# Hybrid decoder block on one core: high-part products first at the head of both networks, squares added in pairs

## The chip, the cores and the metric

The kernel runs on one core of a Trainium2 chip. The metric is the device time of one execution in microseconds (us); the time before is the median of three runs. The engines are TensorE (PE in the rows; its weight loads PEld), VectorE (DVE), ScalarE (ACT), GpSimd (POOL) and SyncE (SP), which issues most DMAs.

## What is computed

A decoder block on 1040 tokens (16 meta tokens and 1024 inputs) of width 1024: a gated network, a middle part, a second gated network, and a last normalization.

```python
def _rmsnorm(x, gain):
    xf = x.astype(jnp.float32)
    y = xf * lax.rsqrt(jnp.mean(xf * xf, axis=-1, keepdims=True) + EPS)
    return (y * gain.astype(jnp.float32)).astype(x.dtype)
def _swiglu(x, w_gu, w_down):
    gate, up = jnp.split(x @ w_gu, 2, axis=-1)
    return (jax.nn.silu(gate) * up) @ w_down
...
h = h + 0.5 * _swiglu(_rmsnorm(h, ffn1_norm[l]), ffn1_w_gu[l], ffn1_w_down[l])
...
h = h + merged @ w_out[l]
h = h + 0.5 * _swiglu(_rmsnorm(h, ffn2_norm[l]), ffn2_w_gu[l], ffn2_w_down[l])
return _rmsnorm(h, final_norm)[:, N_META:]
```

The middle part (a chunked delta-rule branch and an RWKV-7 branch, merged) is not touched. `w_gu` has 2 x 2816 columns, so each network has 22 blocks of 128 gate columns and 22 of up columns, over a contraction of 8 tiles of 128.

## The kernel before

**Products.** A float32 product is made as three products of rounded parts: `split` (L159, L160) makes a high copy on ScalarE and the low rest, source minus high, on VectorE, and TensorE sums high by high, high by low and low by high in PSUM. Weights go through `split` too (`w<-wraw`, `w<-wrx`).

**The networks.** Activations lie with the 1024 features on partitions (8 tiles, `KD`; `HK` = 4 is half of them) and the tokens along the free axis, in two halves of n tokens: n is 520 in the first network (as 256 and 264 columns, `halves`) and 512 in the second. A tile of the first half is called `h` (first network) or `hh` (second); its split form is `b` (`11` and `21`: tiles 0 to 3 and 4 to 7), that of the second half is `12` and `22`, `bt` and `b` in the rows. `gate_up` (L474 and on) does the first pair of units with `plain`: for each half h of the tokens four products (gate of unit 0, gate of unit 1, up of both), each 24 matmuls for every stretch of columns, in an order of all three parts of a tile, tile by tile. Each product has its own PSUM tile (`pg`). From the second pair on `product` (L450) does fewer products by combining halves; its first matmuls are the end of the head.

**The norm.** `rstd` squares a tile on ScalarE (L318), sums over the partitions by a matmul with ones (L320; float32, two records a matmul in the trace, PSUM tile `nps`), over all eight tiles, and makes 1/sqrt by Ln and Exp (L323, L324) into `nrs`. `first_half` multiplies each tile by gain and `nrs` on VectorE (L336) and splits it; `second_half` does the same for the other half (L354). In the second network the statistics of the first half come from elsewhere (L293).

**The order.** `start` interleaves the generators: weights, second half's norm, products. A scheduler places instructions on the engines from that order and from when their inputs should be ready, so parts of the norm lie among products of `plain`. In the second network the products of the attention output (`pwo`, L262) lie on TensorE just ahead; their weights are split by the same two engines, and VectorE adds them up at L898. The tiles of squares, `nrs` and the gates share a pool of six (`ga`). The first loads of `h` go alternately over ScalarE's and SyncE's queues (L648).

Of the kernel before, what the change touches and what calls it, by code (L numbers as in the profile page):

```python
# [300 lines left out]
    return g.ga.tile([P, n], F32, name=name, tag="ga", bufs=6)  # L301


def rstd(g, src, n, on_pe):

    nc = g.nc
    new = lambda: ga_tile(g, n, "nsq")
    if not on_pe:
        r = Rms(g, new, n)
        for k in range(KD):  # L310
            r.add(src(k))
        rs = g.ga.tile([P, n], F32, name="nrs", tag="nrs")
        r.finish(rs)
        return rs
    ps = [g.mx.tile([P, 512], F32, name="nps", tag="mx")[:, :cn] for _, cn in halves(n)]
    for k in range(KD):
        t = new()
        nc.scalar.activation(t, src(k), AF.Square)  # L318
        for p, (c0, cn) in zip(ps, halves(n)):
            nc.tensor.matmul(p, lhsT=g.C("ones"), rhs=t[:, c0 : c0 + cn], start=k == 0, stop=k == KD - 1)  # L320
    rs = ga_tile(g, n, "nrs")
    for p, (c0, cn) in zip(ps, halves(n)):
        nc.scalar.activation(rs[:, c0 : c0 + cn], p, AF.Ln, bias=g.V("eps"), scale=1.0 / D)  # L323
    nc.scalar.activation(rs, rs, AF.Exp, scale=-0.5)  # L324
    return rs
# [4 lines left out]
def first_half(g, hs, gname, n, b, on_pe):  # L330

    src = lambda k: hs[k][:, :n]
    rs = rstd(g, src, n, on_pe)
    yield
    for k in range(KD):
        g.nc.vector.scalar_tensor_tensor(src(k), src(k), g.V(gname, k), rs, op0=ALU.mult, op1=ALU.mult)  # L336
        bk = b["21" if k >= HK else "11"][:, k % HK]
        split(g, src(k), bk[:, 0, :], bk[:, 1, :])
    yield


# [95 lines left out]
def gate_up(g, which, n, w, b):  # L437
# [26 lines left out]
        add(c11, c12, p2)  # L464
        return w, c12, c11

    def plain(l1, r1, l2, r2):
        ps = mm_tile(g, "pg", n)
        for c0, cn in halves(n):
            i = 0  # L470
            for l, r in ((l1, r1), (l2, r2)):
                for k in range(HK):
                    for x, y in ((0, 0), (0, 1), (1, 0)):
                        nc.tensor.matmul(ps[:, c0 : c0 + cn], lhsT=l[:, x, k, :], rhs=r[:, k, y, c0 : c0 + cn],  # L474
                                         start=i == 0, stop=i == 6 * HK - 1)
                        i += 1
        return ps

    def store(x, p, h):
        nc.sync.dma_start(g.hid[p + HF * (h // 2)][:, h % 2 * n : (h % 2 + 1) * n], x)  # L480

    for h in range(2):
        gate = []
        for u in w:
            for m in range(2):
                ps = plain(u[f"{m + 1}1"], b[f"1{h + 1}"], u[f"{m + 1}2"], b[f"2{h + 1}"])
                if len(gate) < 2:
                    x = ga_tile(g, n, "c")
                    nc.scalar.activation(x, ps, AF.Silu)
                    gate.append(x)  # L490
                else:
                    x = gate[m]
                    nc.vector.tensor_tensor(x, ps, x, op=ALU.mult)
                    store(x, 0, 2 * m + h)
        yield
# [116 lines left out]
        f0 += G  # L612


def start(g, which, hs, gname, n, b, w, q):

    more = second_half(g, hs, gname, n, b)
    gu = g.gate_up = gate_up(g, which, n, w, b)
    next(q)
    next(more)  # L620
    next(q)
    next(gu)
    next(more)
# [8 lines left out]
def ffn1(g):  # L632
    tc, nc = g.tc, g.nc
    n = T // 2
    with ExitStack() as ctx:
# [7 lines left out]
        with tc.tile_pool(name="f1n", bufs=1, reuse_waits="tile") as sp:  # L643
            hs = [sp.tile([P, T], F32, name=f"h{k}") for k in range(KD)]
            for s in range(2):
                for k in range(KD):
                    sl = slice(s * n, (s + 1) * n)
                    (nc.sync if s or k % 2 else nc.scalar).dma_start(hs[k][:, sl], g.a["hT"][k][:, sl])  # L648
                if not s:
                    weight_tiles(g)  # L650
                    q0 = whole(g, 1, 0, 0, g.wq[0], g.wq[1])
                    w0 = next(q0)
# [4 lines left out]
            next(q0)  # L657
            next(first)
            next(q0)
            start(g, 1, hs, "g1", n, b, (w0, w1), q1)  # L660
            gu = g.gate_up
        hidden = Hidden(g, ctx.enter_context(tc.tile_pool(name="f1d", bufs=1, reuse_waits="tile")), T)
        with tc.tile_pool(name="gs", bufs=1, reuse_waits="tile") as sp:
# [1032 lines left out]
```

## Time and profile before

| | |
|---|---|
| median of three runs | 3088.84 us (3085.60 to 3089.95) |
| the profiled execution | 3085.29 us, span 3083.5 us, mean granted clock 0.989 |
| TensorE busy | 2959.3 us, 96% of the span |
| VectorE busy | 1976.2 us, 64% |
| ScalarE busy | 1376.7 us, 45% |
| first matmul of a product, first network | 20.30 us |
| first matmul of the second pair of units, first network | 71.90 us |
| first matmul of the first pair, second network | 2394.80 us |
| first matmul of the second pair, second network | 2438.77 us |

All times count from the start of the profiled execution's span. A row of a timeline is a run of instructions of the same kind on one engine: start, length, engine, line, operation, output and input, how many, and in brackets how long the engine stood idle ahead of it and who ended that. The granted clock is given as a share of full speed.

### The profile page before, as it was taken

The page shows a single profiled execution, that of the slowest core. Times are in us where ns is not written, and L with a number is a line of the kernel's source. Part 1 is how long each engine was busy: PE and PEld are TensorE (multiplying, and loading weights), DVE is VectorE, ACT ScalarE, POOL GpSimd, SP SyncE. Part 2 cuts the span into 40 slices and gives each one's busy share as a digit, 9 for nine tenths or more (in the row PEclk, how much of TensorE's full clock was granted, in tenths as well). Part 3 has the DMA queues.
Part 4 walks back from the last instruction along what each step waited for, and adds up shares of the span by engine and source line. Part 5 has one row for each costly group of instructions (what it writes and reads, how often), then busy time and mean ns, then how long its engine had stood idle before and what let it go on. Part 6 is the DMA issues. An engine that isn't in the chain of part 4 may idle for free.

```text
span 3083.5 us, 61656 instructions
## 1 busy us (share of the span) xinstructions
PE 2959.3 (96%) x25498; PEld 2539.0 (82%) x25498; DVE 1976.2 (64%) x3840; ACT 1376.7 (45%) x2404; POOL 354.9 (12%) x519
## 2 busy tenths in 40 slices
PE   8999999999899999999999999999999999999998
PEld 8999998998778888788777777777777888887886
DVE  6455454346677777787867877777866655555335
ACT  5322222126555656566566655665644432222114
POOL 0222220000001000001001000010100022222000
PEclk9999999999899999999999999999999999999999
DMA  3232224234222322333332332223354232224223
GB/s 125 82 97 83 83 86 158 79 101 140 62 74 73 79 70 59 85 79 75 97 89 73 84 81 75 75 75 84 109 148 165 68 104 94 83 83 170 86 78 114
DMA packets 257593, 287.19 MB, mean 93 GB/s; under 512 B 169296, under 2 KB 175440, under 8 KB 257312
## 3 DMA queue, kind: packets, MB, share of 16 engines
q1 hardware_dynamic: 253072, 271.43, 29.4%
q0 software_dynamic: 2512, 8.65, 0.7%
q8 instruction: 201, 3.29, 0.4%
q10 hardware_dynamic: 1728, 3.16, 0.3%
q14 instruction: 80, 0.66, 0.1%
HBM read 232.70 MB, written 50.47 MB: 92 GB/s over the span
## 4 chain that ended last, share of the span: by engine, by line
PE 54%; DVE 11%; ACT 7%; issue 2%; DMA 2%; SPq 0%; DVEq 0%; POOL 0%; ACTq 0%
PE pp L262 18%; PE pg L450 12%; PE pd L262 7%; PE pwo L262 3%; DVE w L160 1%; PE pg L474 1%; PE b L1542 1%; PE cs L1003 1%; PE gra L1252 1%; DMA ugr<-in_upg 1%; PE bkt L1281 1%; DVE tb L1364 1%; DVE mt L1472 1%; DVE Xb L1366 1%; PE vp L1056 1%
## 5 line engine op out<-in xcount | busy, mean ns | idle before, releaser
L262 PE MATMUL pp<-uk,w 128*128 128x512 f32 (+2 forms) x4824 | 975.1, 347 | 15.8 <-DVE w L160 9.3
L262 PEld LDWEIGHTS pp<-uk,w 128*128 128x128 f32 x4824 | 744.7, 191 | 109.1 <-DVE w L160 13.0
L159 ACT ACTIVATE w<-wraw 128x1024 fp32r<-128x1024 f32 (+2 forms) x330 | 326.3, 989 | 712.6 <-PE pd L262 287.6
L262 PE MATMUL pd<-hd,w 128*128 128x512 f32 (+2 forms) x2640 | 495.6, 349 | 11.3 <-DVE w L160 6.7
L262 PEld LDWEIGHTS pd<-hd,w 128*128 128x128 f32 x2640 | 427.5, 189 | 78.2 <-DVE w L160 8.6
L160 DVE TENSOR_TENSOR w<-wraw,w 128x1024 fp32r<-128x1024 f32 (+2 forms) x330 | 376.1, 1140 | 90.9 <-ACT w L159 85.7
L456 DVE TENSOR_TENSOR c<-c,pg 128x520 f32<-128x520 f32 (+1 forms) x280 | 189.2, 689 | 337.3 <-PE pg L450 278.3
L450 PE MATMUL pg<-bt,w 128*128 128x256 f32 (+2 forms) x2520 | 403.9, 317 | 0.0
L450 PEld LDWEIGHTS pg<-bt,w 128*128 128x128 f32 x2520 | 361.0, 188 | 32.9 <-DVE w L160 0.2
L450 PE MATMUL pg<-b,w 128*128 128x256 f32 (+2 forms) x2160 | 348.1, 317 | 0.2 <-DVE c L456 0.2
L450 PEld LDWEIGHTS pg<-b,w 128*128 128x128 f32 x2160 | 309.8, 188 | 28.5 <-PE pg L450 0.4
L419 POOL TENSOR_TENSOR wrx<-wrx 128x512 f32<-128x512 f32 x38 | 57.2, 1505 | 755.1 <-DVE w22b L160 515.3
L1364 DVE TENSOR_TENSOR tb<-Ub,Xb 115x126 f32<-115x126 f32 (+22 forms) x496 | 124.1, 250 | 11.0 <-DMA Ub<-scr 2.7
L1366 DVE TENSOR_TENSOR Xb<-Xb,tb 115x126 f32<-115x126 f32 (+22 forms) x496 | 125.3, 253 | 8.7
L159 ACT ACTIVATE w<-wrx 128x1024 fp32r<-128x1024 f32 (+1 forms) x64 | 58.1, 908 | 156.8 <-PE pg L450 152.3
L1173 DVE SCALAR_TENSOR_TENSOR acc<-xr,pk,acc 128x528 f32<-128x528 f32 (+1 forms) x144 | 109.0, 757 | 26.4 <-ACT acc L1169 25.3
L609 DVE SCALAR_TENSOR_TENSOR h<-pd,h 128x528 f32<-128x528 f32 (+1 forms) x64 | 44.6, 698 | 115.0 <-PE pd L262 115.0
L609 DVE SCALAR_TENSOR_TENSOR hh<-pd,hh 128x512 f32<-128x512 f32 x64 | 44.2, 690 | 109.7 <-PE pd L262 106.6
L262 PE MATMUL pwo<-uk,w 128*128 128x512 f32 x384 | 101.5, 414 | 4.2 <-DVE w L160 1.9
L262 PEld LDWEIGHTS pwo<-uk,w 128*128 128x128 f32 x384 | 73.6, 197 | 22.2 <-DVE w L160 2.7
L923 ACT ACTIVATE sh<-pp,pk 128x528 f32<-128x528 f32 (+1 forms) x54 | 37.5, 694 | 98.3 <-PE pp L262 98.3
L159 ACT ACTIVATE hd<-hr 128x1040 fp32r<-128x1040 f32 (+1 forms) x44 | 45.3, 1061 | 68.6 <-DMA hr<-hid 43.7
(397 smaller groups left out, 4143.1 us busy)
## 6 DMA issues: line engine op xcount, KB each, us to landing
wraw<-in_win SPq DMA_DIRECT2D x150, 512.0 KB
wraw<-in_wgu SPq DMA_DIRECT2D x44, 512.0 KB
wrx<-in_wgu SPq DMA_DIRECT2D x44, 512.0 KB
wraw<-in_wdn SPq DMA_DIRECT2D x48, 320.0 KB
wraw<-in_wdn SPq DMA_DIRECT2D x32, 384.0 KB
hid<-c SPq DMA_DIRECT2D x44, 260.0 KB
hr<-hid SPq DMA_DIRECT2D x22, 520.0 KB
hid<-c SPq DMA_DIRECT2D x44, 256.0 KB
```

What stands on the lines that cost most here:

```text
L159: g.nc.scalar.activation(hi, src, AF.Copy)
L160: (eng or g.nc.vector).tensor_tensor(lo, src, hi.bitcast(F32), op=ALU.subtract)
L262: g.nc.tensor.matmul(ps, lhsT=l, rhs=r, start=i == 0, stop=i == n - 1)
L419: sums.tensor_tensor(a22, a21, a22, op=ALU.add)
L450: nc.tensor.matmul(ps[:, c0 : c0 + cn], lhsT=l[:, x, k, :], rhs=r[:, k, y, c0 : c0 + cn], start=i == 0, stop=i == 3 * HK - 1)
L456: nc.vector.tensor_tensor(o, x, y, op=ALU.add)
L474: nc.tensor.matmul(ps[:, c0 : c0 + cn], lhsT=l[:, x, k, :], rhs=r[:, k, y, c0 : c0 + cn], start=i == 0, stop=i == 6 * HK - 1)
L609: nc.vector.scalar_tensor_tensor(hv, pd, 0.5, hv, op0=ALU.mult, op1=ALU.add)
L923: nc.scalar.activation(sh[:, 1 : 1 + n], ps, AF.Identity, scale=g.V("mu", i))
L1173: nc.vector.scalar_tensor_tensor(acc[:, :n], xr[:, tap : tap + n], V("convw", ct * 4 + tap), acc[:, :n], op0=ALU.mult, op1=ALU.add)
L1364: nc.vector.tensor_tensor(tv, U[:, i, i + 1 :].unsqueeze(2).to_broadcast([npt, nt, ncc]), X[:, i, 0:ncc].unsqueeze(1).to_broadcast([npt, n ...
L1366: nc.vector.tensor_tensor(X[:, i + 1 :, 0:ncc], X[:, i + 1 :, 0:ncc], tv, op=ALU.add)
```

## The change

Four edits. `rstd` takes `pairs`: in the first half of the first network VectorE adds the squares of two tiles, and TensorE sums four tiles where it summed eight. `first_half` does all eight multiplies and high copies first and the eight low parts behind them. `gate_up` begins, for the first half of the tokens, with the high parts of the inputs: products 0 and 1 for all eight tiles in turn (high and low weights by high input), then product 2 so, then the norm of the second half (held behind those products by `issue_after`), then the three products' low passes, then product 3 whole. The load of tile 6's first half goes to SyncE's queue.

```diff
@@ -301,7 +301,7 @@
     return g.ga.tile([P, n], F32, name=name, tag="ga", bufs=6)
 
 
-def rstd(g, src, n, on_pe):
+def rstd(g, src, n, on_pe, pairs=False):
 
     nc = g.nc
     new = lambda: ga_tile(g, n, "nsq")
@@ -316,8 +316,13 @@
     for k in range(KD):
         t = new()
         nc.scalar.activation(t, src(k), AF.Square)
+        if pairs:
+            if k % 2 == 0:
+                even = t
+                continue
+            nc.vector.tensor_tensor(t, even, t, op=ALU.add)
         for p, (c0, cn) in zip(ps, halves(n)):
-            nc.tensor.matmul(p, lhsT=g.C("ones"), rhs=t[:, c0 : c0 + cn], start=k == 0, stop=k == KD - 1)
+            nc.tensor.matmul(p, lhsT=g.C("ones"), rhs=t[:, c0 : c0 + cn], start=k == pairs, stop=k == KD - 1)
     rs = ga_tile(g, n, "nrs")
     for p, (c0, cn) in zip(ps, halves(n)):
         nc.scalar.activation(rs[:, c0 : c0 + cn], p, AF.Ln, bias=g.V("eps"), scale=1.0 / D)
@@ -330,12 +335,15 @@
 def first_half(g, hs, gname, n, b, on_pe):
 
     src = lambda k: hs[k][:, :n]
-    rs = rstd(g, src, n, on_pe)
+    rs = rstd(g, src, n, on_pe, on_pe)
+    yield
+    part = lambda k, i: b["21" if k >= HK else "11"][:, k % HK, i, :]
+    for k in range(KD):
+        g.nc.vector.scalar_tensor_tensor(src(k), src(k), g.V(gname, k), rs, op0=ALU.mult, op1=ALU.mult)
+        g.nc.scalar.activation(part(k, 0), src(k), AF.Copy)
     yield
     for k in range(KD):
-        g.nc.vector.scalar_tensor_tensor(src(k), src(k), g.V(gname, k), rs, op0=ALU.mult, op1=ALU.mult)
-        bk = b["21" if k >= HK else "11"][:, k % HK]
-        split(g, src(k), bk[:, 0, :], bk[:, 1, :])
+        g.nc.vector.tensor_tensor(part(k, 1), src(k), part(k, 0).bitcast(F32), op=ALU.subtract)
     yield
 
 
@@ -464,26 +472,45 @@
         add(c11, c12, p2)
         return w, c12, c11
 
-    def plain(l1, r1, l2, r2):
-        ps = mm_tile(g, "pg", n)
-        for c0, cn in halves(n):
-            i = 0
-            for l, r in ((l1, r1), (l2, r2)):
-                for k in range(HK):
-                    for x, y in ((0, 0), (0, 1), (1, 0)):
-                        nc.tensor.matmul(ps[:, c0 : c0 + cn], lhsT=l[:, x, k, :], rhs=r[:, k, y, c0 : c0 + cn],
-                                         start=i == 0, stop=i == 6 * HK - 1)
-                        i += 1
-        return ps
+    HI, LO = ((0, 0), (1, 0)), ((0, 1),)
+
+    def passes(which, *prods, start=True, stop=True):
+
+
+        for q in range(2):
+            for k in range(HK):
+                for ps, l, r in prods:
+                    for c0, cn in halves(n):
+                        for x, y in which:
+                            m = nc.tensor.matmul(ps[:, c0 : c0 + cn], lhsT=l[q][:, x, k, :],
+                                                 rhs=r[q][:, k, y, c0 : c0 + cn],
+                                                 start=start and (q, k, (x, y)) == (0, 0, which[0]),
+                                                 stop=stop and (q, k, (x, y)) == (1, HK - 1, which[-1]))
+        return m
 
     def store(x, p, h):
         nc.sync.dma_start(g.hid[p + HF * (h // 2)][:, h % 2 * n : (h % 2 + 1) * n], x)
 
     for h in range(2):
         gate = []
+        prod = lambda u, m: (mm_tile(g, "pg", n), [u[f"{m + 1}{i}"] for i in (1, 2)], [b[f"{i}{h + 1}"] for i in (1, 2)])
+        begun = []
+        if h == 0:
+
+            begun = [prod(w[0], 0), prod(w[0], 1)]
+            g.begun = passes(HI, *begun, stop=False)
+            begun.append(prod(w[1], 0))
+            passes(HI, begun[2], stop=False)
+            yield
         for u in w:
             for m in range(2):
-                ps = plain(u[f"{m + 1}1"], b[f"1{h + 1}"], u[f"{m + 1}2"], b[f"2{h + 1}"])
+                if begun:
+                    p = begun.pop(0)
+                    passes(LO, p, start=False)
+                else:
+                    p = prod(u, m)
+                    passes(HI + LO, p)
+                ps = p[0]
                 if len(gate) < 2:
                     x = ga_tile(g, n, "c")
                     nc.scalar.activation(x, ps, AF.Silu)
@@ -612,12 +639,16 @@
         f0 += G
 
 
-def start(g, which, hs, gname, n, b, w, q):
+def start(g, which, hs, gname, n, b, w, q, first=iter(())):
+
 
     more = second_half(g, hs, gname, n, b)
     gu = g.gate_up = gate_up(g, which, n, w, b)
     next(q)
-    next(more)
+    next(gu)
+    next(first, None)
+    with g.tc.issue_after(g.begun.ins):
+        next(more)
     next(q)
     next(gu)
     next(more)
@@ -645,7 +676,7 @@
             for s in range(2):
                 for k in range(KD):
                     sl = slice(s * n, (s + 1) * n)
-                    (nc.sync if s or k % 2 else nc.scalar).dma_start(hs[k][:, sl], g.a["hT"][k][:, sl])
+                    (nc.sync if s or k % 2 or k == 6 else nc.scalar).dma_start(hs[k][:, sl], g.a["hT"][k][:, sl])
                 if not s:
                     weight_tiles(g)
                     q0 = whole(g, 1, 0, 0, g.wq[0], g.wq[1])
@@ -657,7 +688,7 @@
             next(q0)
             next(first)
             next(q0)
-            start(g, 1, hs, "g1", n, b, (w0, w1), q1)
+            start(g, 1, hs, "g1", n, b, (w0, w1), q1, first)
             gu = g.gate_up
         hidden = Hidden(g, ctx.enter_context(tc.tile_pool(name="f1d", bufs=1, reuse_waits="tile")), T)
         with tc.tile_pool(name="gs", bufs=1, reuse_waits="tile") as sp:
```

In the rows that follow `nsq` is a tile of squares, `ones` the matrix of ones, `pg` a product, `b_103` and `b_102` the split tiles 0 to 3 and 4 to 7 of the first half, `w` weights. TensorE, head of the first network, before (the sum of the first half ends with the first row; each row of `nps` is one stretch of columns of a tile):

```order
L320 MATMUL nps<-nsq,ones 128x264
L320 MATMUL nps<-nsq,ones 128x256
L320 MATMUL nps<-nsq,ones 128x264
L320 MATMUL nps<-nsq,ones 128x256
L320 MATMUL nps<-nsq,ones 128x264
L474 MATMUL pg<-b_103,w 128x256 x2
L474 MATMUL pg<-b_103,w_133 128x256
L320 MATMUL nps<-nsq,ones 128x256
L320 MATMUL nps<-nsq,ones 128x264
L474 MATMUL pg<-b_103,w 128x256 x6
L320 MATMUL nps<-nsq,ones 128x256
L320 MATMUL nps<-nsq,ones 128x264
```

and after, from the first half's last pair of tiles; the products of all high parts stand in a row behind (more such rows up to the next fence):

```order
L325 MATMUL nps<-nsq,ones 128x256
L325 MATMUL nps<-nsq,ones 128x264
L485 MATMUL pg<-b_103,w 128x256 x2
L485 MATMUL pg<-b_103,w 128x264 x2
L485 MATMUL pg<-b_103,w 128x256 x2
L485 MATMUL pg<-b_103,w 128x264 x2
L485 MATMUL pg<-b_103,w 128x256 x2
```

The second half's sum begins, after the change, behind 96 product matmuls, at the end of product 2's high parts:

```order
L485 MATMUL pg<-b_102,w_133 128x256 x2
L485 MATMUL pg<-b_102,w_133 128x264 x2
L325 MATMUL nps<-nsq,ones 128x256
L325 MATMUL nps<-nsq,ones 128x264
L325 MATMUL nps<-nsq,ones 128x256
L325 MATMUL nps<-nsq,ones 128x264
```

Before, sums of the second half's squares were spread among the first product's matmuls and ahead of it; now all of them stand in one row behind the high parts of three products.

VectorE, head of the second network, before (`hh` input tiles, `b` their split forms, `w<-wraw,w` the low part of a `pwo` weight tile):

```order
L336 SCALAR_TENSOR_TENSOR hh_27128<-hh_27128,pk,nrs 128x512
L336 SCALAR_TENSOR_TENSOR hh_27129<-hh_27129,pk,nrs 128x512
L160 TENSOR_TENSOR b_27115<-hh_27126,b_27115 128x512
L160 TENSOR_TENSOR b_27116<-hh_27127,b_27116 128x512
L160 TENSOR_TENSOR b_27116<-hh_27128,b_27116 128x512
L160 TENSOR_TENSOR b_27116<-hh_27129,b_27116 128x512
L336 SCALAR_TENSOR_TENSOR hh_27130<-hh_27130,pk,nrs 128x512
L160 TENSOR_TENSOR w<-wraw,w 128x1024
L160 TENSOR_TENSOR b_27116<-hh_27130,b_27116 128x512
L898 TENSOR_TENSOR hh_27126<-pwo,hh_27126 128x512
```

and after:

```order
L342 SCALAR_TENSOR_TENSOR hh_27126<-hh_27126,pk,nrs 128x512
L346 TENSOR_TENSOR b_27111<-hh_27119,b_27111 128x512
L346 TENSOR_TENSOR b_27111<-hh_27120,b_27111 128x512
L346 TENSOR_TENSOR b_27111<-hh_27121,b_27111 128x512
L346 TENSOR_TENSOR b_27111<-hh_27122,b_27111 128x512
L346 TENSOR_TENSOR b_27112<-hh_27123,b_27112 128x512
L346 TENSOR_TENSOR b_27112<-hh_27124,b_27112 128x512
L346 TENSOR_TENSOR b_27112<-hh_27125,b_27112 128x512
L346 TENSOR_TENSOR b_27112<-hh_27126,b_27112 128x512
L160 TENSOR_TENSOR w<-wraw,w 128x1024
L929 TENSOR_TENSOR hh_27122<-pwo,hh_27122 128x512
```

The weights' low part stood ahead of one low part of the inputs; now it stands behind all eight.

TensorE, head of the second network, before:

```order
L262 MATMUL pwo<-uk,w 128x512 x23
L320 MATMUL nps<-nsq,ones 128x512 x2
L262 MATMUL pwo<-uk,w 128x512 x2
L320 MATMUL nps<-nsq,ones 128x512
L262 MATMUL pwo<-uk,w 128x512 x94
L320 MATMUL nps<-nsq,ones 128x512 x5
L474 MATMUL pg<-b_27115,w 128x512 x12
L474 MATMUL pg<-b_27116,w 128x512 x12
L474 MATMUL pg<-b_27115,w 128x512 x12
L474 MATMUL pg<-b_27116,w 128x512 x12
```

and after:

```order
L293 MATMUL nps<-nsq,ones 128x512
L262 MATMUL pwo<-uk,w 128x512 x119
L485 MATMUL pg<-b_27111,w 128x512 x9
L485 MATMUL pg<-b_27112,w 128x512 x2
L485 MATMUL pg<-b_27111,w 128x512 x7
L485 MATMUL pg<-b_27112,w 128x512 x14
L485 MATMUL pg<-b_27111,w_27470 128x512 x8
L485 MATMUL pg<-b_27112,w_27470 128x512 x8
L325 MATMUL nps<-nsq,ones 128x512 x8
L485 MATMUL pg<-b_27111,w 128x512 x4
L485 MATMUL pg<-b_27112,w 128x512 x4
```

The sums of the second half's squares stood in three places, two of them between the products of `pwo`; now `pwo` is in one row and all eight sums stand behind the high parts of three products.

## Rows read from the trace of the kernel before

**Rows 1.** Timeline of TensorE, 0 to 75 us; columns as told above.

```profile
6.72 9.44 PE L320 MATMUL nps<-nsq,ones 128*128 128x256 f32 x32 [6.72 <-DMA ones<-in_ck]
16.80 2.04 PE L320 MATMUL nps<-nsq,ones 128*128 128x256 f32 x8 [0.64 <-ACT nsq L318]
20.30 0.62 PE L474 MATMUL pg<-b,w 128*128 128x256 f32 x3 [1.46 <-ACT b L159]
...
22.52 3.67 PE L320 MATMUL nps<-nsq,ones 128*128 128x256 f32 x16
...
71.90 3.26 PE L450 MATMUL pg<-b,w 128*128 128x256 f32 x26
```

**Rows 2.** Windows: stretch, us, busy (count) PE PEld DVE ACT POOL, granted clock, DMA.

```profile
7.00:9.00 2.00, 2.00 (x5) 1.52 (x5) 0.40 (x4) 1.26 (x4) 0.00 (x0) 1.00 1.05 405
13.00:15.00 2.00, 2.00 (x11) 1.73 (x10) 1.75 (x2) 1.01 (x2) 0.00 (x0) 1.00 1.05 392
...
866.00:868.00 2.00, 2.00 (x11) 2.00 (x10) 2.00 (x6) 0.83 (x3) 0.00 (x0) 0.53 0.87 291
...
2366.00:2368.00 2.00, 0.96 (x2) 0.84 (x3) 2.00 (x3) 0.51 (x1) 0.00 (x0) 0.59 0.00 0
...
2396.00:2442.00 46.00, 46.00 (x205) 38.06 (x204) 39.07 (x61) 22.62 (x37) 0.00 (x0) 1.00 0.13 49
...
31.00:72.00 41.00, 41.00 (x344) 41.00 (x344) 33.70 (x53) 20.09 (x32) 0.00 (x0) 1.00 0.11 41
...
2442.00:2452.00 10.00, 10.00 (x46) 8.28 (x45) 6.34 (x7) 5.19 (x7) 0.00 (x0) 1.00 0.17 54
```

**Rows 3.** Timeline of ScalarE and its DMA issues (ACTq), 0 to 30 us.

```profile
0.78 4.22 ACTq L648 DMA_DIRECT2D h<-in_hT  x4
...
8.32 1.16 ACT L318 ACTIVATE nsq<-h 128x520 f32<-128x520 f32 x2 [0.73 <-DMA h<-in_hT]
10.96 0.64 ACT L318 ACTIVATE nsq<-h 128x520 f32<-128x520 f32 x1 [1.47 <-DMA h<-in_hT]
...
15.75 0.47 ACT L323 ACTIVATE nrs<-nps,pk 128x256 f32<-128x256 f32 x1 [1.74 <-PE nps L320]
...
19.63 0.62 ACT L159 ACTIVATE b<-h 128x520 fp32r<-128x520 f32 x1
```

**Rows 4.** Timeline of VectorE, 0 to 40 us.

```profile
18.21 2.10 DVE L336 SCALAR_TENSOR_TENSOR h<-h,pk,nrs 128x520 f32<-128x520 f32 x3 [2.94 <-DMA wraw<-in_wgu]
```

**Rows 5.** Timeline of TensorE at the head of the second network, 2354 to 2460 us.

```profile
2359.77 1.88 PE L320 MATMUL nps<-nsq,ones 128*128 128x512 f32 x4
...
2367.04 24.03 PE L262 MATMUL pwo<-uk,w 128*128 128x512 f32 x92 [1.86 <-DVE w L160]
2390.91 4.45 PE L320 MATMUL nps<-nsq,ones 128*128 128x512 f32 x10
2394.80 19.65 PE L474 MATMUL pg<-b,w 128*128 128x512 f32 x84
...
2455.09 2.88 PE L450 MATMUL pg<-b,w 128*128 128x512 f32 x12
```

**Rows 6.** Timeline of VectorE at the head of the second network, 2354 to 2456 us.

```profile
2366.90 0.68 DVE L160 TENSOR_TENSOR b<-hh,b 128x512 fp32r<-128x512 f32 x1
...
2396.79 0.75 DVE L354 SCALAR_TENSOR_TENSOR hh<-hh,pk,nrs 128x512 f32<-128x512 f32 x1 [3.31 <-ACT nrs L324]
...
2451.23 1.22 DVE L160 TENSOR_TENSOR w<-wrx,w 128x1024 fp32r<-128x1024 f32 x1
```

**Rows 7.** Timeline of TensorE: four of the five idle times above 2.5 us.

```profile
815.51 2.04 PE L1211 MATMUL grb<-AR,BK 64*64 64x128 f32 x32 [2.59 <-DVE LT L1214]
...
864.54 5.70 PE L262 MATMUL pp<-uk,w 128*128 128x272 f32 x32 [2.73 <-DVE w L160]
...
1531.81 8.46 PE L262 MATMUL pp<-uk,w 128*128 128x512 f32 x36 [3.40 <-DVE gg L1582]
1664.76 6.60 PE L262 MATMUL pp<-uk,w 128*128 128x512 f32 x17 [2.83 <-DVE w L160]
```

## The prediction

> **What bounds the kernel now.** I read the page's busy line first: TensorE is busy for nearly the whole span, so a change gains only where TensorE stands idle, runs below its rate, or does work that can go. Next comes TensorE's timeline at the head of the first network [rows 1]; the reader should look at the bracket behind each row, the idle time ahead of it. TensorE sums squares until 6.72 + 9.44 = 16.2 us, and the first product starts at 20.30 us, released by ScalarE's high copy of the first input tile. From there to 71.90 us it runs almost without a gap: the stretch from 31 to 72 us is 41.00 us busy of 41.00 [rows 2], and the second pair of units starts at 71.90 us [rows 1]. So the start of the first product and the work behind it set the time. ScalarE's and VectorE's rows [rows 3, 4] tell why the start is at 20.30. At the second network TensorE still has the products of the attention output (`pwo`) to do while the inputs are made; no row there waits for an input tile, and what it waits for are weights (1.86 us for VectorE's low part) [rows 5]. Last I read the granted clock [rows 2], since the change moves idle time.
>
> **First network, the start.** Before, ScalarE issues four of the first loads until 0.78 + 4.22 = 5.0 us, and squares tile 6 only at 10.96 us (it waited for the load) and tile 7 behind a weight copy [rows 3]. Now one load goes out on the other queue and all eight squares stand ahead of the weight copies. Six squares are done at 8.32 + 1.16 = 9.5 us as now; I put tiles 6 and 7 right behind them, 0.52 us each, at 10.5 us, and the last of the four new VectorE additions, taken as long as a subtraction of the same 128x520 floats (0.69 us, from 2.10 us for three slower multiplies as the upper end 0.70 [rows 4]), ends at 11.2 us. Then four matmul records are left. In the sum of squares there are 32 records in 9.44 us; the window at 7 us holds 5 in 2 us (0.40 us each), the one at 13 us holds 11 (0.18 us each) [rows 1, 2]. Four records thus end between 12.0 and 12.8 us; I take 12.5, near the slow end, since records wait in a row from 6.72 us on.
>
> The profile's clock column says 1.00 in both windows, while the matmuls of the first go at half the rate [rows 2]. The Trainium skill ("TensorE: Matmul & The Clock Gate", Part 1, What's actually happening) says that the default is the throttled state and that activity releases it; by that rule the early records are at 1.2 GHz whatever the column says, and the rows agree with the rule, not with the column. By the column the sum would end at 12.0, by the rule at 12.8; the total moves by 0.8 us at most.
>
> From the end of the sum to the first product it is 20.30 − 16.16 = 4.1 us before: two Ln from 15.75, Exp, the first multiply at 18.21, and the copy `b`, which stood behind a weight copy until 19.63 [rows 3, 4]. That weight copy is gone from the way, but two squares of the second half (2 × 0.52 us) stand between Exp and the copy. Ends: 3.7 us (weight copy gone, squares hidden) and 4.6 us; I take 4.0. First product: 12.5 + 4.0 = **16.5 us**, 3.8 us earlier (16.0 to 17.3).
>
> **First network, behind the start.** Before, 20.30 to 71.90 us holds 384 product matmuls and 24 sum records: two of the eight second-half tiles were summed at 16.80 us, in the gap [rows 1]. From 26.9 us on, 374 matmuls take 45.0 us, 0.120 us each (41.00/344 = 0.119 in the window [rows 2]); 384 make 46.2 us. A sum record takes 0.197 us (16 from 22.52 to 25.84, less one product matmul of 0.12 and rounding [rows 1]), 24 make 4.7. The remaining 0.7 us are waits. Now all eight tiles, 32 records, 6.3 us, stand in the stretch: 1.6 us more; the waits go, as high products of a tile take TensorE 8 × 0.12 = 0.96 us while VectorE makes a tile in 0.70 us. So 16.5 + 46.2 + 6.3 = 69.0 us instead of 71.90.
>
> **The clock.** TensorE now stands still from 12.5 to 16.5 us. The trace has five idle times above 2.5 us behind its start; the rows show four of them, 2.59, 2.73, 3.40 and 2.83 us [rows 7]. Behind the one of 3.40 us 36 matmuls of 512 columns took 8.46 us (0.235 each, full rate); behind that of 2.83 us 17 took 6.60 (0.39 each), and behind that of 2.73 us the granted clock was 0.53 [rows 2, 7], half (1.2 of 2.4 GHz). Half clock followed four of the five. At the second network 1.86 us was enough (0.59 at 2366 us [rows 2]). So I expect a fall. Cost: at 2367.04 us 92 matmuls take until 2390.91, 23.9 us, where 92 × 0.224 (46.00/205 [rows 2]) would be 20.6: **3.2 us** lost [rows 5]; behind 864.54 us half clock lasts until about 868, so 3.5 us at 0.53, 1.6 us lost. I take 2.0, nearer to the short one, since that too began with a plain idle time. First network: 69.0 + 2.0 − 71.90 = **−0.9 us** (−2.9 without a fall, +0.3 with the dear one).
>
> The second half is made later: its multiply starts at about 35.8 us (sum at 28.2 to 34.5, then Ln and Exp). It is needed when the low products and product 3 are done (96 matmuls of 0.12, to 46 us), and eight tiles at 1.35 us with other work between them end at 48; tile 7 is needed at about 51. VectorE has cover of 3 us; no cost.
>
> **Second network.** Products of high parts first bring no earlier start, since the products of `pwo` lie ahead anyway. Three things change. (a) Before, six of sixteen sum records (the first four at 2359.77 us [rows 5]) lay in the gap in which TensorE waited for weights; now all sixteen stand among the products. Ten take 2394.80 − 2390.91 = 3.89 us [rows 5], so six add **+2.3 us**. (b) The low part of the fifth `pwo` weight tile, which TensorE waits for until 2367.04, stood ahead of the last of eight low parts, which starts at 2366.90 and takes 0.68 us [rows 6]; now it stands behind that one: **+0.6 us** (0 to 0.7). (c) The clock: TensorE is idle longer in that gap, so it should fall earlier; the half-clock stretch that costs 3.2 us can cost as little as 1.6: **−0.8** (0 to −1.6). Together **+2.1 us** (+0.7 to +3.0).
>
> VectorE gets a backlog there: the second-half multiply starts after the high products (48 × 0.224 = 10.8 us), all sixteen records (6.2) and Ln and Exp (2.0), counted from the end of `pwo` (2390.91 + 0.6 − 0.8): at about 2409.7 instead of 2396.79 us [rows 6], 12.9 us later. From 2396 to 2442 VectorE is busy 39.07 of 46 us and TensorE never idle [rows 2]; 6.9 us of idle time, and 3.7 us more from 2442 to 2452 us (6.34 of 10 busy), can take up most of it, and what is needed next (low weights made at 2451.23 + 1.22 = 2452.5 us [rows 6] for products at 2455.09 [rows 5]) has 2.6 us of room. I cost it at nothing; the upper end is the slow rival.
>
> **Sum.** −0.9 + 2.1 = +1.2 us. The profiled execution took 3085.29 us (span 3083.5): 3086.5 us. It is 3.55 us under the median of the three runs, 3088.84, so the forecast is 3090.0 us.
>
> **Rivals.**
> *The clock holds.* If TensorE keeps full clock over the 4 us at 12.5 us, as it did at 1531 us, the first network gains 2.9, and the total is 2.1 − 2.9 = −0.8: 3088.0 us. If it also holds at the second network (−3.2 instead of −0.8), 3085.6. For: one of the five idle times. Against: the other four.
> *Slower: VectorE's backlog at the second network.* If its idle times there are waits for TensorE that move along with it, it catches up less than it needs. It decides from 12.9 − 2.6 = 10.3 us: what it catches up short of that, TensorE waits in the second pair of units. Catching up nothing gives +1.2 + 10.3 = 3100.3; half gives 3095.2, the edge of slower. For: its 3.31 us of idle time ahead of 2396.79 us ends with another engine's work [rows 6], and so may the others. Against: 6.9 + 3.7 = 10.6 us of idle time are there.
> *Faster by more.* The rest of the program is the same, but all of it starts at another instant, and the clock's falls elsewhere depend on the instant: 2.73 us brought one, 3.40 us did not. Two falls fewer at 3.2 us each and the held clock: 3081.6. As likely the other way.
> *It does not do what it says.* If the loads set the squares (tile 6 still landing near 10.9 us), the sum ends at 13.5 and the first product at 17.5: +1.0, 3091.0, within the range.
>
> **How the numbers follow.** Forecast as summed 0.62; clock holds 0.17; backlog 0.12; faster by falls gone 0.04; more falls, or the late load, 0.05. A measurement of this kernel can tell about 0.2%, 6.2 us, from no change (3082.7 to 3095.0). Forecast, late load and held clock lie within; of the backlog about two thirds lie beyond, of the rest most. Faster 0.07, same 0.80, slower 0.13. Range: the runs of before spread by ±2.2 us and the terms by −2.5 to +2; with the held clock below and the cheap half of the backlog above it is 3084.5 to 3096.
>
> **What would show it.** First product near 16.5 us, sum of squares ending near 12.5; granted clock near 0.5 for 3 to 6 us behind that; the second pair of units at about 71.0 us instead of 71.90. At the second network `pwo` without sums among its products, TensorE back at 2367.6 on the old scale, 16 sum records behind the high products, no idle TensorE to the second pair of units. The forecast is wrong if TensorE waits for VectorE or for weights behind either head, or if matmuls that change their PSUM tile at every second step go slower than 0.12 and 0.224 us.

## The result: 0.18% slower, 3.1 us of it at the second head

Over 22 runs of each kernel the changed one takes 3093.86 us in the median (3086.95 to 3098.02) and the kernel before 3086.93 us (3083.76 to 3093.60). The ratio is 1.0018, 95% interval 1.0012 to 1.0024, or +5.6 us (+3.7 to +7.4); the two medians lie 6.9 us apart. The forecast was +1.2 us. The profiled execution of the changed kernel took 3086.95 us, the shortest of its 22 (span 3085.2 us), so the two profiles alone show only +1.7 us. Below, a head's length is read from the start times of rows, called stamps. One run of the changed kernel in the table below, 3274 us at a mean clock of 0.843, was in a slower state of the chip and is left out.

TensorE's timeline of the changed kernel, first network (start, length, engine, line, operation, count, in brackets the idle time ahead and who ended it):

```profile
8.94 5.48 PE L325 MATMUL nps<-nsq,ones 128*128 128x256 f32 x16 [8.94 <-DVE nsq L323]
18.06 13.43 PE L485 MATMUL pg<-b,w 128*128 128x256 f32 x96 [3.64 <-ACT b L343]
31.32 7.18 PE L325 MATMUL nps<-nsq,ones 128*128 128x256 f32 x32
38.14 8.86 PE L485 MATMUL pg<-b,w 128*128 128x256 f32 x72
...
72.75 2.43 PE L458 MATMUL pg<-b,w 128*128 128x256 f32 x19
```

VectorE and ScalarE there:

```profile
7.89 0.18 DVE L132 TENSOR_SCALAR pk<-pk 128x27 f32<-128x27 f32 x1 [6.99 <-DMA pk<-in_pk]
...
8.19 1.95 DVE L323 TENSOR_TENSOR nsq<-nsq 128x520 f32<-128x520 f32 x3
10.50 0.70 DVE L323 TENSOR_TENSOR nsq<-nsq 128x520 f32<-128x520 f32 x1 [0.35 <-ACT nsq L318]
...
8.25 2.22 ACT L318 ACTIVATE nsq<-h 128x520 f32<-128x520 f32 x4 [0.95 <-DMA h<-in_hT]
```

And the granted clock (stretch, us, busy us and count of each engine, then clock, DMA share, GB/s):

```profile
18.00:20.00 2.00, 1.94 (x13) 1.94 (x14) 2.00 (x4) 2.00 (x5) 0.00 (x0) 0.81 1.04 416
20.00:22.00 2.00, 2.00 (x11) 2.00 (x10) 2.00 (x4) 2.00 (x4) 0.00 (x0) 0.50 0.12 45
```

Against [rows 1] the first product comes 2.2 us earlier (18.06 for 20.30), not 3.8, and the second pair of units 0.85 us later (72.75 for 71.90). The sums start at 8.94 us, where TensorE could sum from 6.72 before: VectorE's first addition stands in its queue behind four small operations on the constants, which wait until 7.89 us for their load. Then half clock: 96 products take 13.26 us (18.06 to 31.32) where 96 × 0.120 would be 11.5.

TensorE at the head of the second network, one row of the kernel before, then the changed kernel; the last two rows are a row of TensorE's weight loads (PEld) and one of VectorE:

```profile
2354.11 5.82 PE L262 MATMUL pwo<-uk,w 128*128 128x512 f32 x23
...
2351.96 5.83 PE L262 MATMUL pwo<-uk,w 128*128 128x512 f32 x23
...
2365.49 23.73 PE L262 MATMUL pwo<-uk,w 128*128 128x512 f32 x92 [2.46 <-DVE w L160]
2389.07 11.26 PE L485 MATMUL pg<-b,w 128*128 128x512 f32 x48
2400.17 7.03 PE L325 MATMUL nps<-nsq,ones 128*128 128x512 f32 x16
2406.63 8.74 PE L485 MATMUL pg<-b,w 128*128 128x512 f32 x36
...
2439.69 11.04 PE L458 MATMUL pg<-b,w 128*128 128x512 f32 x48
...
2453.93 2.14 PEld L458 LDWEIGHTS pg<-bt,w 128*128 128x128 f32 x10 [0.46 <-DVE w L160]
...
2408.62 4.07 DVE L362 SCALAR_TENSOR_TENSOR hh<-hh,pk,nrs 128x512 f32<-128x512 f32 x6 [10.12 <-ACT nrs L329]
```

From the fourth `pwo` tile's products to the second pair of units it takes 2439.69 − 2351.96 = 87.73 us, before 2438.77 − 2354.11 = 84.66. A second profile of the kernel before (the last experiment) gives 84.63. The difference is 3.1 us: sixteen sum records take 6.46 us in the stretch (2400.17 to 2406.63) where ten took 3.89 [rows 5], +2.6; the wait for the weight's low part ends 13.53 us behind the fourth tile's start, 12.93 before, +0.6; the 92 `pwo` products are 0.3 shorter, the products behind them 0.2 longer.

### The profile page after: what moved, and what is told of

Read it like the earlier page. It is cut to its first block, busy times and chain, and to the rows that moved or that the text cites. A ratio compares the mean times of both kernels' runs of the same rounds, so it can differ in the third digit from the quotient of the medians.

```text
span 3085.2 us, 61631 instructions
## 1 busy us (share of the span) xinstructions
PE 2957.4 (96%) x25482; PEld 2538.8 (82%) x25482; DVE 1977.2 (64%) x3844; ACT 1376.3 (45%) x2404; POOL 353.6 (11%) x519
## 4 chain that ended last, share of the span: by engine, by line
PE 55%; DVE 11%; ACT 6%; issue 2%; DMA 1%; DVEq 0%; POOL 0%; SPq 0%; ACTq 0%
PE pp L262 18%; PE pg L458 12%; PE pd L262 7%; PE pwo L262 3%; DVE w L160 2%; PE pg L485 1%; PE b L1573 1%; PE cs L1034 1%; PE gra L1283 1%; DVE tb L1395 1%; PE bkt L1312 1%; DVE Xb L1397 1%; PE vp L1087 1%; DMA ugr<-in_upg 1%; DVE mt L1503 1%
## 5 line engine op out<-in xcount | busy, mean ns | idle before, releaser
L262 PE MATMUL pp<-uk,w 128*128 128x512 f32 (+2 forms) x4824 | 976.5, 347 | 15.2 <-DVE w L160 9.3
L262 PEld LDWEIGHTS pp<-uk,w 128*128 128x128 f32 x4824 | 745.8, 191 | 108.4 <-DVE w L160 12.9
```

The costliest lines, as they stand in the source:

```text
L262: g.nc.tensor.matmul(ps, lhsT=l, rhs=r, start=i == 0, stop=i == n - 1)
```

## The experiments

**Which head it is.** One head as changed, the other as before, and the changed kernel again (the diffs of this part are cut to the lines that matter).

```diff
-    next(gu)
-    next(first, None)
-    with g.tc.issue_after(g.begun.ins):
-        next(more)
+    if which in (1,):        # e2: (2,), and no pairs, no moved load
+        next(gu)
+        next(first, None)
+        with g.tc.issue_after(g.begun.ins):
+            next(more)
+    else:
+        next(more)
```

(In the network that is left out, `first_half` and the products are those of before.)

> First network as changed, second network as before. Theory A (the cost is the sum of the two heads): the second pair of units of the first network starts at 72.7 +- 0.5 us as in the changed kernel (71.90 before), the second network's head takes 2.87 us less than in the changed kernel; time over before +0.9 us (0 to +2.5). Rival B (the change shifts the falls of the clock in the middle of the program, and that is where most of the time goes): about +4 us, as the start of everything is moved as in the changed kernel. Rival C (VectorE's backlog in the second network): +0.9 us, like A.

> First network as before, second network as changed. Theory A: from the end of the attention output's fourth weight tile to the second pair of units the head takes 3.1 us longer than before, of it 2.6 for six more sum records among the products and 0.6 for the low weight behind one more low part; time over before +3.1 us (+2 to +5). Rival B: about 0 to +3, half clock in the middle as before. Rival C: TensorE idle behind 2439 us waiting for VectorE, by more than 1 us in the second pair of units, +3 to +6.

> The changed kernel itself once more, for a second profile. Theory A: the heads take the same as in the first profile to 0.5 us but for the clock (72.75 and 2439.69 - 2351.96 = 87.7 us from the fourth weight tile's products to the second pair of units), and the half clock elsewhere differs; +4 us over before (+3 to +7). Rival B: the heads the same, and more half clock in the middle part than in the profile of before: total loss to half clock 42 us or more against 34. Rival C: idle TensorE waiting for VectorE behind the second network's head.

Eleven runs of each, beside 33 of the kernel before:

| kernel | ratio to before (95%) | us | second pair, first network | fourth tile to second pair, second network |
|---|---|---|---|---|
| only the first head changed | 0.9998 (0.9988 to 1.0009) | −0.6 (−3.7 to +2.8) | 74.09 | 84.62 |
| only the second head changed | 1.0015 (1.0006 to 1.0023) | +4.6 (+1.9 to +7.1) | 73.15 | 87.93 |
| changed, again | 1.0018 (1.0009 to 1.0027) | +5.6 (+2.8 to +8.3) | 74.22 | 87.76 |

TensorE's timeline with only the first head changed, then of the changed kernel's second profile:

```profile
18.70 14.12 PE L491 MATMUL pg<-b,w 128*128 128x256 f32 x96 [3.64 <-ACT b L349]
...
74.09 1.10 PE L464 MATMUL pg<-b,w 128*128 128x256 f32 x8
```

```profile
8.78 6.40 PE L325 MATMUL nps<-nsq,ones 128*128 128x256 f32 x16 [8.78 <-DVE nsq L323]
18.82 14.13 PE L485 MATMUL pg<-b,w 128*128 128x256 f32 x96 [3.64 <-ACT b L343]
...
2360.44 5.82 PE L262 MATMUL pwo<-uk,w 128*128 128x512 f32 x23
...
2448.20 1.98 PE L458 MATMUL pg<-b,w 128*128 128x512 f32 x8
```

The second head repeats: 87.7 to 87.9 us as changed in three profiles, 84.5 to 84.7 as before in eight of nine profiles, and 83.31 in the ninth, where half clock behind the wait was shorter. The first takes 71.83 to 73.15 us as before (three profiles) and 72.75 to 74.22 as changed (four), between −0.4 and +2.4 us and +1.5 in the mean. The forecast of 72.7 ± 0.5 for the kernel with only the first head changed missed: against the first profile its first product came 0.6 us later and its 96 products lost 0.7 us more to half clock. Theory A holds: the second head carries most of it, and the two together, +4.6 us in the mean of the profiles (+2.7 to +5.5), agree with the measured +5.6 (+3.7 to +7.4). The times of the first two kernels in the table are too wide to split it on their own; the stamps do.

The rival by VectorE's backlog (C) all but falls. VectorE begins the second half at 2408.62 us, and TensorE's rows from 2406 to 2450 us show no idle time. But at 2453.93 us a weight load has waited 0.46 us for a low part that VectorE ends at 2453.88, 0.54 and 0.52 in the two other profiles with the sums held; TensorE's 24 products there take 0.3 to 0.45 us longer than the 5.44 us of the kernel before, and 5.44 again where the norm is not held (the next experiment). That lies behind the stamp and comes on top of the 3.1 us.

Rival B, the clock in the middle part, set itself a mark of 42 us lost to half clock, against 34 in the first profile of the kernel before. Taken as span times what is missing of the mean granted clock, the second profile of the changed kernel has 46 us (mean clock 0.985, span 3096.6 us) and so meets it. But the mark was drawn from one profile: the 33 runs of the kernel before that go with it lose 38 us in the mean, ten runs of the changed kernel 43. Of these 4.6 us the heads explain about 4: behind the first product the clock is half for 3.4 to 6.8 us (0 to 3.4 before), at the second head for 10.2 (6.8 before), and half of that counts as lost. So no price of the middle part is needed; one of 1 or 2 us is not excluded. What the middle part does is spread the runs. In the stretch from 816 to 830 us the same code had, in the changed kernel's two profiles (spans 3085.2 and 3096.6 us):

```profile
816.00:830.00 14.00, 10.02 (x190) 7.92 (x190) 6.33 (x17) 4.05 (x12) 0.10 (x1) 1.00 0.33 82
```

```profile
816.00:830.00 14.00, 11.32 (x156) 9.29 (x158) 5.71 (x17) 1.39 (x4) 0.10 (x1) 0.51 0.26 59
```

The clock is full once and half the other time. The idle time at its beginning is 2.59 us in both, ended by the same tile of VectorE. Such falls come and go between executions: the two profiles of the changed kernel, 11.4 us apart, lose 34 and 46 us to the clock. The first, the shortest of its runs, has the mean clock of the profile before (0.989 both); that is why these two alone differ by 1.7 us where the medians differ by 6.9.

**The sums back in the gap of the second network.**

```diff
-    next(gu)
-    next(first, None)
-    with g.tc.issue_after(g.begun.ins):
+    if which in (1,):              # held, as in the changed kernel
...
+    else:                          # second network: not held
         next(more)
+        if which in (1, 2):
+            next(gu)
+            next(first, None)
```

> The changed kernel, but in the second network the second half's norm is no longer held behind the products of high parts, so that three sums of eight fall into the gap among the attention output's products, as before. Theory A: six records of 0.40 us leave the busy stretch, the head is 2.5 us shorter than in the changed kernel; +1.5 us over before (0.5 to 4). Rival B: no difference to the changed kernel beyond 1 us in the total. Rival C: VectorE starts the second half some 10 us earlier, so any wait of TensorE for it goes as well, and the gain is more than 2.5 us.

Ratio 1.0013 (1.0004 to 1.0022), +4.0 us; the head takes 84.81 us:

```profile
2357.45 5.82 PE L262 MATMUL pwo<-uk,w 128*128 128x512 f32 x23
2363.11 2.74 PE L325 MATMUL nps<-nsq,ones 128*128 128x512 f32 x6
...
2370.98 23.58 PE L262 MATMUL pwo<-uk,w 128*128 128x512 f32 x92 [2.94 <-DVE w L160]
...
2442.26 8.10 PE L458 MATMUL pg<-b,w 128*128 128x512 f32 x35
```

2.9 us of the 3.1 are back in the head, with the wait for the weight as late as in the changed kernel (13.53 us behind the fourth tile). So the sums' place is the price at the second head. The total came at the upper edge of its forecast (0.5 to 4 us) and, by the ratios, 1.5 us under the changed kernel, with intervals that overlap; the stamps carry this too.

**What holds the first head's start.** Four variants, all with the second network as before, one execution each, so that only their stamps are read. Without pairs; with VectorE's operations on the constants behind the additions; with the second half's norm not held; with idle time filled by matmuls of the matrix of ones whose results are not used.

```diff
-    rs = rstd(g, src, n, on_pe, on_pe)
+    rs = rstd(g, src, n, on_pe)                        # e5
+    if pairs:                                          # e6, and not at the start of build
+        with g.tc.issue_after(last.ins): g.prep()
-    with g.tc.issue_after(g.begun.ins):
+    next(more)                                         # e7, ahead of next(gu)
+    with g.tc.issue_after(end.ins):                    # e8, and 4 ahead of the sums
+        for i in range(14):
+            nc.tensor.matmul(idle[:, :P], lhsT=g.C("ones"), rhs=g.C("ones"), start=True, stop=True)
```

> First network as changed but without the pairs (TensorE sums all eight tiles of the first half), second network as before. Theory D (the pairs cost more than they save: VectorE's additions stand behind four small operations that wait for a load until about 7.9 us, so TensorE starts its sums at 8.7 us instead of 6.7): sums start at 6.6 +- 0.3 us, end at 13.0 +- 0.7, first product at 17.0 +- 0.7 instead of 18.7. Rival E (the sum ends with the last square whatever the pairs do): sums end at 15.1 us and the first product comes at 18.7 +- 0.3.

> First network as changed, with the pairs, but VectorE's four small operations on the constants stand behind the pairs' additions; second network as before. Theory D: sums start at 6.7 +- 0.3 us and end at 12.8 +- 0.6 (11.2 for the last pair plus four records), first product at 16.5 +- 0.6. Rival E: no change, 15.1 and 18.7 us.

> First network as changed but the second half's norm is not held behind the products of high parts, so that four sums of its eight fall into the gap between the first half's sum and the first product; second network as before. Theory F (the gap with an idle TensorE brings the half clock behind it): no granted clock under 0.9 from 19 to 26 us, 96 high-part products at 0.12 us, and 16 of 32 sum records out of the busy stretch: second pair of units at 70.5 +- 1 us against 74.1. Rival G (the half clock at 16 to 26 us is the one that the execution starts with and passes at a time of its own): still half clock to about 25 us, second pair at 72 +- 0.7.

> First network as changed, with 4 matmuls of the matrix of ones by itself ahead of the first sums and 14 behind them, whose results are not used; second network as before. Theory F: TensorE is busy from 6.7 us to the first product, the clock is full at the first product (18.7 us), and the second pair of units starts at 71.5 +- 0.7 instead of 74.1 us. Rival G: half clock to about 25 us as before, second pair at 74 +- 0.5 us.

TensorE, in this order, each from its first sums to the second pair of units:

```profile
6.46 9.26 PE L325 MATMUL nps<-nsq,ones 128*128 128x256 f32 x32 [6.46 <-DMA ones<-in_ck]
19.36 13.40 PE L491 MATMUL pg<-b,w 128*128 128x256 f32 x96 [3.64 <-ACT b L349]
...
74.03 6.25 PE L464 MATMUL pg<-b,w 128*128 128x256 f32 x51
```

```profile
6.51 6.28 PE L327 MATMUL nps<-nsq,ones 128*128 128x256 f32 x16 [6.51 <-DVE nsq L325]
17.03 13.18 PE L496 MATMUL pg<-b,w 128*128 128x256 f32 x96 [4.24 <-ACT b L354]
...
71.47 8.76 PE L469 MATMUL pg<-b,w 128*128 128x256 f32 x72
```

```profile
16.02 3.97 PE L325 MATMUL nps<-nsq,ones 128*128 128x256 f32 x16 [0.65 <-ACT nsq L318]
19.62 0.72 PE L491 MATMUL pg<-b,w 128*128 128x256 f32 x3
...
69.47 10.80 PE L464 MATMUL pg<-b,w 128*128 128x256 f32 x89
```

```profile
14.45 3.29 PE L333 MATMUL pg<-ones 128*128 128x128 f32 x28
17.81 11.93 PE L499 MATMUL pg<-b,w 128*128 128x256 f32 x96
...
71.01 9.23 PE L472 MATMUL pg<-b,w 128*128 128x256 f32 x76
```

```profile
22.00:24.00 2.00, 2.00 (x19) 2.00 (x18) 2.00 (x4) 2.00 (x5) 0.00 (x0) 1.00 0.00 0
```

(The last row is the window of the variant with idle time filled.) Without pairs the sum ends at 15.72 us, not 13.0: 32 records need 9.26 us without a gap, the first ten 0.43 us apart or a little more and the others 0.22, while the last square is done at 11.98 us. So TensorE's records bind it, not the squares. My theory D was wrong there: the pairs do save 0.66 us to the first product (18.70 for 19.36), though at the second pair of units nothing is left of it (74.03 and 74.09), as half clock was shorter without them.

With the constants behind the additions, sixteen records run from 6.51 to 12.79 us and the first product comes at 17.03: 1.7 us earlier, and D is right for the wait. The other 0.9 us of the 2.6 to the second pair (71.47) is again less half clock. The chain behind became 4.24 instead of 3.64 us, as ScalarE was still at the weight copies.

Theory F holds in both its tests: with four sums of the second half in the gap, or with matmuls that do nothing, the clock is 1.00 behind the first product. With the latter 96 high-part products take 11.8 us (17.81 to 29.58, the next row's start) instead of 13.0 to 14.0 in the six profiles that have the idle time. The useful filling gives 69.47 us, the idle one 71.01, against 74.09 with neither; 0.9 of the idle one's 3.1 us is an earlier first product, the rest the clock.

**Both mends, and the weight's wait.** The constants behind the additions and the norm not held; then also, in the second network, the first half's multiplies and splits issued behind the fifth `pwo` tile.

```diff
-            for _ in first_half(g, hs, "g2", n, b, False):
-                pass
+            first = first_half(g, hs, "g2", n, b, False)
+            next(first)
             for m, ho in wout(g, g.mg, lambda m: hs[m][:, n:]):
                 nc.sync.dma_start(g.h3dr[m], ho)
+                if m == 4:
+                    next(first)
```

> First network as changed, with VectorE's four small operations behind the pairs' additions and the second half's norm not held behind the products of high parts; second network as before. Theory D and F together: first sums from 6.6 to 12.9 us, sums of the second half in the gap behind them, no half clock behind the first product, second pair of units at 68 +- 1 us (71.90 and 73.15 us in the two profiles with the first head as before); time over before -4 us (-6.5 to -1.5). Rival E/G: second pair at 69.5 to 72, time -1 to -3 us.

> The same, and in the second network the first half's multiplies and splits are issued behind the fifth weight tile of the attention output, so that the weight's low part stands behind 5 multiplies and 3 low parts instead of 8 and 7. Theory H (that wait for VectorE is on the path in both kernels): from the fourth tile's products to the ones behind the wait 8.5 +- 1 us instead of 12.9, and less half clock behind it; a further -4.5 us and up to -3 for the clock: -9 us over before (-12 to -6). Rival I (another release, as ScalarE's high part or a load, comes right behind): less than 1.5 us further.

Both mends, 11 runs beside 15 of the kernel before: ratio 0.9985 (0.9976 to 0.9994), −4.6 us; second pair of the first network at 66.94 us. With the weight's wait as well, 5 runs: 0.9959 (0.9947 to 0.9972), 3073.17 us in the median, −12.7 us, more than the forecast (−6 to −12). TensorE with both mends, then VectorE, TensorE and the granted clock of the last kernel at its second head:

```profile
13.68 3.96 PE L327 MATMUL nps<-nsq,ones 128*128 128x256 f32 x16 [0.68 <-ACT nsq L320]
17.28 0.71 PE L496 MATMUL pg<-b,w 128*128 128x256 f32 x3
...
66.94 9.23 PE L469 MATMUL pg<-b,w 128*128 128x256 f32 x76
```

```profile
2354.95 1.22 DVE L162 TENSOR_TENSOR w<-wraw,w 128x1024 fp32r<-128x1024 f32 x1
...
2347.09 5.83 PE L264 MATMUL pwo<-uk,w 128*128 128x512 f32 x23
...
2356.25 21.92 PE L264 MATMUL pwo<-uk,w 128*128 128x512 f32 x94
...
2424.98 11.04 PE L469 MATMUL pg<-b,w 128*128 128x512 f32 x48
...
2356.00:2372.00 16.00, 16.00 (x70) 12.88 (x69) 10.04 (x14) 6.14 (x9) 0.00 (x0) 1.00 0.47 149
```

The low part of the weight ends at 2356.17 us, as the sums in the gap end, TensorE doesn't wait, the clock stays, and the head takes 77.89 us instead of 84.66: −6.8. This version beats both kernels, and over half of its gain comes from a wait that the kernel before had too and that the change had made longer.

**What the order of high parts is worth.** The products in the order of before, with the pairs, the moved load and the constants behind the additions; and the kernel before again.

```diff
-        if h == 0:
+        if h == 0 and which in ():
```

> The products of both networks in the order of before, all parts of a tile together; only the pairs, the load on the other queue and VectorE's four small operations behind the pairs' additions. Theory J (the high parts first are worth little, the earlier sum is what gains): first product at 17.3 +- 0.5 us as in the run with both mends, second pair of units at 67.7 +- 0.7 us against its 66.94. Rival K (with tiles wanted whole, TensorE waits between them while VectorE makes multiply and low part in turn): second pair at 69.5 us or later, by waits of 2 us and more between 17 and 27 us.

> The kernel before once more, for a second whole profile of its heads. Theory A: from the fourth weight tile's products of the attention output to the second pair of units of the second network 84.7 +- 0.3 us (84.66 in the first profile), first network's second pair of units between 71.9 and 73.2 us, where the difference is half clock at 20 to 24 us. Rival B: differences of more than 1 us in the second head, so that a single profile can't carry the sum.

TensorE of the first kernel, then of the kernel before:

```profile
17.39 0.59 PE L531 MATMUL pg<-b,w 128*128 128x256 f32 x2
...
67.35 8.88 PE L469 MATMUL pg<-b,w 128*128 128x256 f32 x73
```

```profile
71.83 4.45 PE L464 MATMUL pg<-b,w 128*128 128x256 f32 x36
...
2356.90 5.83 PE L262 MATMUL pwo<-uk,w 128*128 128x512 f32 x23
...
2441.53 8.78 PE L464 MATMUL pg<-b,w 128*128 128x512 f32 x38
```

Second pair at 67.35 us without the high parts first (one profile), 66.94 and 67.00 with them (the two kernels with both mends): 0.4 us. Rival K's waits did not come: TensorE's rows from 17.39 us on show no idle time. The rest of the 5 us comes from the earlier sum and from the gap filled with sums. Both kernels have the sums not held, so this does not show what the order is worth with them held.

## Why the prediction was right, and where it was off

The range held, the direction was right, and "within 0.2%" came true barely: +0.18%. The likeliest value was 4.4 us too low. In the direction there was luck: the first network was forecast faster (−0.9 us) and came slower (+1.5 in the mean of the profiles); only the second network's price made the sum come out as slower. The absolute forecast was helped too, as its base, the median of three runs, was 1.9 us above the median of 22.

- **First network, the start: the step that failed.** Tiles 6 and 7 were squared by 10.47 us and the last addition ended at 11.20, as forecast (10.5 and 11.2). But I let only four records be left then, "since records wait in a row from 6.72 us on". They didn't run from 6.72: VectorE's queue held the additions behind the constants, the records began at 8.94 us, and at 11.20 eleven of the sixteen were left. The sum ended at 14.42 (15.06 to 15.2 in the other profiles) instead of 12.5. I had read the order of the additions, not what stood ahead of them on VectorE; the rivals had a late load, but of the wrong tile.
- **From the sum to the first product** 4.0 us were taken, 3.64 measured.
- **First network, behind the start.** The 32 sum records took 6.82 us (31.32 to 38.14), 6.3 forecast. The waits did go.
- **The clock** fell behind the idle time as forecast: 1.8 us lost in the first profile, 2.4 to 2.5 in the three other profiles of that head by the same sum, 2.0 taken. That the idle time brings it was shown by filling it, with sums and with unused matmuls. One reading was too simple: "1.86 us was enough" at the second network leaves out that TensorE had stood idle 1.47 us shortly before.
- **Second network.** (a) +2.3 forecast, +2.6 measured; (b) +0.6, +0.6; (c) −0.8, −0.3: the clock did fall earlier, at 2360.8 us (2366.4 before), but it rose only at 2371.0 (2373.2), so the half clock under the products was hardly shorter. Together +2.1 against +3.1. The mechanism held; c was mis-sized.
- **VectorE's backlog** was costed at nothing and cost 0.3 to 0.45 us. Counted from the fourth `pwo` tile, VectorE began the second half 14.0 us later than before (12.9 forecast). The 2.6 us of room were misread: the products that need the low weights begin within the row at 2449.65, whose fifteenth matmul starts at 2452.82, 0.4 us behind the weights (2452.45), and not at 2455.09.
- **The rule of the Trainium skill** ("TensorE: Matmul & The Clock Gate", Part 1, What's actually happening), that the default is the throttled state, bore out: in the variant with the constants behind the additions the first eleven records start 0.42 us apart or more, the last five 0.22, and the clock column says 1.00 over both:

```profile
7.00:11.00 4.00, 4.00 (x10) 2.64 (x10) 1.85 (x3) 2.75 (x6) 0.00 (x0) 1.00 1.04 404
11.50:12.80 1.30, 1.29 (x6) 0.76 (x4) 1.03 (x2) 1.07 (x2) 0.00 (x0) 1.00 1.05 392
```

## What to carry to other kernels

Before work is moved to an idle engine, read what stands ahead of it in that engine's queue: small operations that wait for a load delayed a chain on which everything waited. Sums that filled a gap on the busiest engine cost nothing here, and at the first head they kept its clock; held behind the products, they cost 2.6 us at one head and left an idle time with half clock behind it at the other. For small changes compare the stamps of the stage that is touched over several profiles: those of the second head repeat to 0.2 us in eleven of twelve, where whole runs spread by 10.

## What was not expected of the hardware

The first float32 sum records of TensorE's work start 0.43 us apart and later ones 0.22, while the clock column reads 1.00 for both. The step came at 11.2 us in the kernel before, whose records begin at 6.72, and in the changed kernel at 12.4 us in one profile and 14.1 in the other, with records from 8.94 and 8.78 us on. So a larger share of the sixteen records ran at half rate: all 32 records without pairs took 9.26 us, the sixteen with pairs still 5.5 to 6.5. The granted clock falls elsewhere in the program in some executions and not in others, for the same code behind the same idle time of 2.59 us: 0.51 and 1.00 from 816 to 830 us.
